# Layer 1's memory keys inside layer 0, the first retention values by token tile, sparse pairs ahead of the memory group

## The chip, the core and the metric

The kernel runs on one core of a Trainium2 chip. The metric is the device time of one execution in microseconds. Three runs of the kernel before gave 436.51 to 436.9 us, with a median of 436.82.

## What is computed

Two layers of a decoder over 256 positions (SEQ) with a model width of 1024, everything in float32. Layer 0 has three groups of heads beside each other: native sparse attention with 8 heads in two key groups (compressed blocks, selected blocks and a window; at 256 positions the selected blocks and the window both see all past tokens), block attention with 8 heads, and memory attention with 4 heads into 256 memory tokens. Layer 1 has retention with 4 heads (256 wide queries and keys, 512 wide values, a group norm over each head) and memory attention again. Each group has a gate path, each layer one output projection and a residual, and a final norm follows. Cut to what matters here:

```python
def memory_attention(q, mem_n, w_mem_kv):
    k, v = jnp.split(mem_n @ w_mem_kv, 2, axis=-1)
    ...
    s = jnp.einsum('bthd,bmhd->bhtm', q, k).astype(jnp.float32) * (HEAD_DIM ** -0.5)
    p = jax.nn.softmax(s, axis=-1).astype(v.dtype)
    return jnp.einsum('bhtm,bmhd->bthd', p, v).reshape(Bsz, T, MEM_W)
...
def odd_layer(x, mem_n, rcos, rsin, norm_g, w_in, w_mem_kv, w_out):
    h = rms_norm(x, norm_g)
    rq, rk, rv, rz, eq, ez = _split(h @ w_in, ODD_SPLITS)
    ...
    v = rv.reshape(Bsz, T, RET_HEADS, RET_V_DIM)
    r_out = head_group_norm(retention(q, k, v)).reshape(Bsz, T, RET_V_W).astype(x.dtype)
    m_out = memory_attention(eq.reshape(Bsz, T, MEM_HEADS, HEAD_DIM), mem_n, w_mem_kv)
```

The memory's keys and values of layer 1 depend on the memory and its weights alone, not on layer 0. The retention's values depend on x after layer 0 (called x1 below).

## The kernel before, in words

**Precision.** A float32 product is made of three matmuls in the format fp32r: the operand is split into a high part (ScalarE casts it, `whi`, line 122) and a low part (VectorE subtracts, `wlo`, line 123), and `mm3` (lines 135 to 137) adds high x high, high x low and low x high. `project_wide` (lines 181 and 182) does the same with two matmuls, of 512 and of 256 columns, for layer 1's turned projections.

**Weights.** They stream from memory through 6 buffers `raw` of 128 x 1024 numbers, loaded on SP's queue, and through 4 buffers each of `whi` and `wlo`. One buffer full is a unit; a projection of 512 columns has four units. A buffer comes free when the last matmul that reads it is done.

**Accumulators.** The eight PSUM banks are given out by tag: three for projections (`pj`), two for scores (`s`), one for transposes of probabilities (`t`), one for outputs of pairs (`o`) and one more (`tr`).

**Layer 0.** The projections run first, for the most part, each over both token tiles of 128 rows. Then come the pairs: a sparse pair has two heads and two branches, and a branch is a chain of scores (line 100), masked maximum and exponential (lines 415 and 417), division, three transposes per head (line 216), ScalarE's copy `pt` (line 430, or 476 for the memory group), and the product with the values (line 100). A pair ends with the gate (lines 441 to 443), which writes its part of the rows `yn`, `ym` or `yb` of the output projection. Five pieces of that projection, two units each, are taken as their rows are ready: `yn` of pairs 0 and 1, `ym`, `yn` of pairs 2 and 3, `yb` of block pairs 0 and 1 and of 2 and 3.

**Between the layers.** For each token tile and half of the columns, VectorE adds the residual (line 757) and multiplies by the norm's gain (line 759), TensorE transposes (line 216), ScalarE casts the high part (line 762) and VectorE subtracts the low part (line 763) of x1. Then `memory_keys1` projects the memory's keys and values for layer 1 (one projection of 512 columns of which the first 256 give the keys and the rest the values), and layer 1's memory queries and gate (`e1`) follow, the retention's queries and keys of heads 0 and 1, and for each head values (`rv`), gate (`rz`) and the retention itself.

**What sets the order.** The program is written in the order above, but a planner reorders it at build time: for every engine it takes, at each moment of its own model of the time, the first instruction in program order whose operands and buffers are ready. Each engine then runs its list strictly in order. `side_by_side` keeps a group of small matmuls together, and `after` lets the first of them wait for other instructions. In `pair_scores` these are the last reads of the scores before (`read`), except for sparse pair 2 and the memory group of layer 0 (`whole` is false). In `sparse_pair`, pair 2 alone gives its first branch's values to TensorE before the second branch is done.

## Time and profile before

| | us |
|---|---|
| median of three runs | 436.82 |
| profiled execution | 436.53 |
| its span, first to last instruction | 434.7 |
| TensorE busy (97% of the span) | 422.0 |
| TensorE's weight loads (81%, beside the matmuls) | 352.2 |
| VectorE busy (73%) | 315.3 |
| ScalarE busy (58%) | 250.5 |
| weights and inputs read | 72.74 MB |

The span is what the trace holds; the profiled execution is 1.8 us longer than that. In the trace's rows the engines are PE (TensorE), PEld (its weight loads), DVE (VectorE), ACT (ScalarE), POOL and SP, a row names the line of the kernel, the operation, what is written and read, and the shape. A matmul's time in such a row includes its way through the array, so that matmuls overlap: the pace is read from one start to the next. Two records stand for one float32 matmul of the pairs.

### The profile page before, as it was taken

How to read it: one execution, taken by the hardware profiler on the slowest of the kernel's cores; microseconds unless marked ns; L12 is line 12 of the kernel's file. 1: busy time of each engine (PE TensorE's matmuls, PEld its weight loads, DVE VectorE, ACT ScalarE, POOL GpSimd, SP SyncE). 2: the span in 40 equal slices, each digit the busy share in tenths (PEclk: the TensorE clock that was granted, in tenths of full speed). 3: DMA queues.
4: the chain of work that ended last, by engine and by line, in shares of the span. 5: the costliest groups of instructions: out<-in, count | busy, mean ns of one | idle time of the engine just before them, and what ended most of it. 6: DMA issues, size and time to landing. Idle time of an engine off the chain costs nothing.

```text
span 434.7 us, 6745 instructions
## 1 busy us (share of the span) xinstructions
PE 422.0 (97%) x2444; PEld 352.2 (81%) x2444; DVE 315.3 (73%) x735; ACT 250.5 (58%) x464; POOL 3.5 (1%) x9
## 2 busy tenths in 40 slices
PE   7999999999999998999999999999999999999994
PEld 6978999889777666669988878888888888888883
DVE  4889787798776786549688875596898557675634
ACT  5585546667858696647457534645445544644703
POOL 0000000000000000000000000000000000000001
PEclk9999999999999999999999999999999999999998
DMA  7975966763434623333663644555466455655202
GB/s 241 397 267 159 342 205 193 264 216 103 149 113 148 236 83 100 96 98 102 189 211 98 193 147 145 194 163 192 148 186 196 155 187 183 206 174 177 75 2 97
DMA packets 30337, 74.22 MB, mean 171 GB/s; under 512 B 2912, under 2 KB 14432, under 8 KB 30304
## 3 DMA queue, kind: packets, MB, share of 16 engines
q1 hardware_dynamic: 29872, 73.40, 51.7%
q8 instruction: 19, 0.31, 0.3%
q10 hardware_dynamic: 432, 0.40, 0.3%
q14 instruction: 14, 0.11, 0.1%
HBM read 72.74 MB, written 1.05 MB: 170 GB/s over the span
## 4 chain that ended last, share of the span: by engine, by line
PE 91%; DMA 4%; ACT 2%; DVE 1%; issue 1%; SPq 0%; DVEq 0%; ACTq 0%
PE pj L135 19%; PE pj L136 19%; PE pj L137 18%; PE pj L181 9%; PE pj L182 4%; PE t L216 4%; PE s L100 4%; PE o L100 3%; DMA raw<-in_w 2%; DMA v<-in_xtok 2%; PE tr L136 1%; PE tr L137 1%; PE tr L135 1%; PE s L136 1%; PE s L137 1%; PE s L135 1%
## 5 line engine op out<-in xcount | busy, mean ns | idle before, releaser
L123 DVE TENSOR_TENSOR wlo<-raw,whi 128x1024 fp32r<-128x1024 f32 (+3 forms) x127 | 147.3, 1166 | 58.9 <-ACT whi L122 57.4
L122 ACT CAST whi<-raw 128x1024 fp32r<-128x1024 f32 (+3 forms) x127 | 126.8, 1003 | 89.7 <-PE pj L137 39.8
L136 PE MATMUL pj<-wlo,big 128*128 128x512 f32 (+2 forms) x264 | 99.4, 377 | 0.0
L137 PE MATMUL pj<-whi,big 128*128 128x512 f32 (+2 forms) x264 | 98.3, 374 | 0.0
L135 PE MATMUL pj<-whi,big 128*128 128x512 f32 (+2 forms) x264 | 98.0, 375 | 0.0
L137 PEld LDWEIGHTS pj<-whi,big 128*128 128x128 f32 x264 | 49.7, 188 | 8.9 <-issue 0.7
L135 PEld LDWEIGHTS pj<-whi,big 128*128 128x128 f32 x264 | 49.6, 188 | 8.7 <-issue 0.4
L181 PE MATMUL pj<-big,whi 128*128 128x512 f32 x160 | 56.5, 396 | 0.0
L136 PEld LDWEIGHTS pj<-wlo,big 128*128 128x128 f32 x264 | 49.7, 188 | 8.4 <-issue 0.3
L182 PE MATMUL pj<-big,wlo 128*128 128x256 f32 x160 | 44.6, 283 | 0.0
L181 PEld LDWEIGHTS pj<-big,whi 128*128 128x128 f32 x160 | 29.8, 188 | 6.7 <-DVE tmp L365 0.3
L135 PE MATMUL pj<-big,whi 128*128 128x256 f32 x120 | 34.4, 290 | 0.1
L136 PE MATMUL pj<-big,whi 128*128 128x256 f32 x120 | 33.9, 285 | 0.0
L137 PE MATMUL pj<-big,wlo 128*128 128x256 f32 x120 | 33.2, 285 | 0.0
L182 PEld LDWEIGHTS pj<-big,wlo 128*128 128x128 f32 x160 | 30.2, 189 | 0.7 <-issue 0.3
L135 PEld LDWEIGHTS pj<-big,whi 128*128 128x128 f32 x120 | 23.0, 192 | 1.3 <-issue 0.7
L417 ACT ACTIVATE p<-p,mx 128x128 f32<-128x128 f32 (+1 forms) x48 | 21.4, 447 | 3.9 <-DVE mx L415 3.8
L136 PEld LDWEIGHTS pj<-big,whi 128*128 128x128 f32 x120 | 23.0, 192 | 0.1
L137 PEld LDWEIGHTS pj<-big,wlo 128*128 128x128 f32 x120 | 22.5, 191 | 0.0
L216 PE MATMUL t<-cst,p 128*128 128x128 f32 x104 | 17.9, 282 | 1.2 <-ACT pt L430 1.2
L216 PEld LDWEIGHTS t<-cst,p 128*128 128x128 f32 x104 | 11.8, 140 | 7.1 <-ACT pt L430 2.3
L430 ACT COPY pt<-t 128x384 f32<-128x384 f32 x24 | 11.4, 476 | 10.6 <-PE t L216 10.4
(302 smaller groups left out, 640.1 us busy)
## 6 DMA issues: line engine op xcount, KB each, us to landing
raw<-in_w SPq DMA_DIRECT2D x91, 512.0 KB, 4.2
raw<-in_wout SPq DMA_DIRECT2D x28, 512.0 KB, 3.8
v<-in_xtok SPq DMA_DIRECT2D x4, 512.0 KB, 8.2
raw<-in_w SPq DMA_DIRECT2D x4, 280.0 KB, 3.5
v<-in_w SPq DMA_DIRECT2D x2, 512.0 KB, 7.6
raw<-in_memT SPq DMA_DIRECT2D x2, 512.0 KB, 4.5
raw<-in_memtok SPq DMA_DIRECT2D x2, 512.0 KB, 4.8
v<-in_grow SPq DMA_DIRECT2D x2, 512.0 KB, 5.8
```

What stands on the lines that cost most here:

```text
L100: ins = PE.matmul(out, lhs, rhs, start=start, stop=stop, skip_group_check=bool(shared))
L122: S.copy(hi, raw)
L123: V.tensor_tensor(lo, raw, hi.bitcast(F32), ALU.subtract)
L135: PE.matmul(ps, lh, rh, start=start, stop=False, skip_group_check=shared)
L136: PE.matmul(ps, lh, rl, start=False, stop=False, skip_group_check=shared)
L137: PE.matmul(ps, ll, rh, start=False, stop=stop, skip_group_check=shared)
L181: PE.matmul(ps[ct], wh[:, c], both[:, :, kt], start=kt == 0, stop=False, skip_group_check=True)
L182: PE.matmul(ps[ct][:, T:], wl[:, c], both[:, 0, kt], start=False, stop=kt == KT - 1, skip_group_check=True)
L216: PE.transpose(b[:, i * P : (i + 1) * P], a, ident)
L417: S.activation(p[:, hh, a], p[:, hh, a], AF.Exp, bias=mx[:, hh, tok : tok + 1], scale=-1.0, accum_out=sm[:, hh, tok : tok + 1])
L430: got = S.copy(pt[:, hh, :384], transposes([p[:, hh, i * P : (i + 1) * P] for i in range(3)]))
```

## The change

1. The projection of layer 1's memory keys and values is cut in two halves of 256 columns (`project_half`, which loads half the columns of each weight row, in pieces of 1 KB). The keys (`memory_keys1`) move to the end of layer 0's program, behind the block pairs and ahead of the output projection. The values (`memory_values1`) stay where both were.
2. The retention's values of head 0 are projected right behind them, ahead of `e1`, and token tile by token tile: `project_rows` splits all four units, then runs tile 0 over all of the depth, then tile 1. The other heads' values keep their place and form.
3. Sparse pair 3 moves ahead of the memory group and the last two block projections. In every sparse pair both branches' values go to TensorE in one group, and every pair's scores wait for the last read of the scores before.
4. The output projection of layer 0 takes the piece of sparse pairs 2 and 3 ahead of the memory group's.

```diff
--- before.py
+++ after.py
@@ -165,6 +165,19 @@
             turned_unit(ps, lhs, wh, wl, (kt, kt + 1), range(4))
         return ps
 
+    def project_rows(src, idx, lhs, cols=512):
+
+        hi, lo = lhs
+        ps = [bank("pj") for _ in range(2)]
+        ws = list(units(src, idx, cols))
+        for tok in range(2):
+            ts = slice(tok * P, (tok + 1) * P)
+            for k0, wh, wl in ws:
+                for j in range(2):
+                    cs = slice(j * cols, (j + 1) * cols)
+                    mm3(ps[tok], hi[:, k0 + j, ts], lo[:, k0 + j, ts], wh[:, cs], wl[:, cs], k0 + j == 0, k0 + j == KT - 1)
+        return ps
+
     def project_wide(src, idx, both):
 
 
@@ -200,6 +213,29 @@
                     c = slice(j * 512 + 256, j * 512 + 512)
                     mm3(ps[1][:, tok * T : (tok + 1) * T], hi[:, kt, ts], lo[:, kt, ts], wh[:, c], wl[:, c],
                         kt == 0 and tok == 0, kt == KT - 1, True)
+        return ps
+
+    def halves(src, idx, half):
+
+        for u in range(2):
+            raw = load(tl("raw", [P, 1024], NRAW),
+                       src[idx + u].rearrange("p (k c) -> p k c", k=4)[:, :, half * 256 : half * 256 + 256])
+            wh, wl = split(raw, 1024)
+            for j in range(4):
+                yield 4 * u + j, wh[:, j * 256 : (j + 1) * 256], wl[:, j * 256 : (j + 1) * 256]
+
+    def project_half(src, idx, lhs, half):
+
+        hi, lo = lhs
+        ps = bank("pj")
+        for kt, wh, wl in halves(src, idx, half):
+            for i in range(2):
+                c = slice(i * P, (i + 1) * P)
+                out = ps[:, i * T : (i + 1) * T]
+                if half == 0:
+                    mm3(out, wh[:, c], wl[:, c], hi[:, kt], lo[:, kt], kt == 0 and i == 0, kt == KT - 1, True)
+                else:
+                    mm3(out, hi[:, kt, c], lo[:, kt, c], wh, wl, kt == 0 and i == 0, kt == KT - 1, True)
         return ps
 
     def spread(col, dst):
@@ -397,11 +433,11 @@
 
     read = []
 
-    def pair_scores(q, k, spans, whole=True):
+    def pair_scores(q, k, spans):
 
         s = [bank("s") for _ in range(2)]
         side_by_side([(s[hh][:, a], q[pair_half(hh), tok * P : tok * P + P], k[pair_half(hh), : a.stop - a.start], True, True)
-                      for tok, a in enumerate(spans) for hh in range(2)], *(read if whole else ()))
+                      for tok, a in enumerate(spans) for hh in range(2)], *read)
         read.clear()
         return [[s[hh][:, a] for a in spans] for hh in range(2)], s
 
@@ -456,7 +492,7 @@
             pt = tl("pt", [P, 2, 512], 2)
             mx = tl("mx", [P, 2, 2], 3)
             sm = tl("sm", [P, 2, 2], 3)
-            _, ss = pair_scores(eqT[:, pr], kT[:, pr], WHOLE, together)
+            _, ss = pair_scores(eqT[:, pr], kT[:, pr], WHOLE)
             for hh in range(2):
                 s = ss[hh]
                 V.tensor_reduce(mx[:, hh], s.rearrange("p (a k) -> p a k", a=2), AX.X, ALU.max, negate=True)
@@ -596,14 +632,11 @@
         PE.matmul(o[:, :T], vcR[:, pr % 2].rearrange("p g f -> p (g f)"), pcT[:, pr // 2], start=True, stop=False)
         todo, done = [], []
         for br in (1, 2):
-            pt, got = causal_weights(pair_scores(nq[:, pr], kS[:, br - 1], SPAN, pr not in (2,))[0],
+            pt, got = causal_weights(pair_scores(nq[:, pr], kS[:, br - 1], SPAN)[0],
                                      gates[:, :, br * 8 + 2 * pr : br * 8 + 2 * pr + 2])
             todo += causal_values(pt, lambda g, kt, br=br: vsw[:, kt, (br - 1) * P + g * 64 : (br - 1) * P + g * 64 + 64],
                                   o, False, br == 2)
             done.append(got)
-            if br == 1 and pr not in (0, 1, 3):
-                side_by_side(todo, *done)
-                todo, done = [], []
         side_by_side(todo, *done)
         gated(o, szn[:, pr], yn, pr)
 
@@ -681,10 +714,16 @@
             gated(o[:, i * T : (i + 1) * T], szb[:, pr], yb, pr)
 
     def memory_keys1():
-        nonlocal mh, ml, rstdm, rbm, k1m, v1m
+        nonlocal k1m
         k1m = tl("s2", [P, 2, T], NS)
+        scaled(project_half(w512, W["m1"], (mh, ml), 0), rbm, 1.0, k1m)
+
+    def memory_values1():
+        nonlocal v1m
         v1m = tl("s2", [P, 2, T], NS)
-        mem_keys(project_mem(w512, W["m1"], (mh, ml)), rstdm, rbm, k1m, v1m)
+        ps = project_half(w512, W["m1"], (mh, ml), 1)
+        for tok in range(2):
+            S.activation(v1m[:, tok], ps[:, tok * T : (tok + 1) * T], AF.Copy, scale=rstdm[:, tok : tok + 1])
 
 
     sparse_keys()
@@ -695,18 +734,18 @@
     block_gates()
     block_keys()
     memory_rows()
-    for pr in range(3):
+    for pr in range(4):
         sparse_pair(pr)
     memory_scale()
     memory_keys()
     memory_group()
     block_queries()
     block_values()
-    sparse_pair(3)
     block_pairs(0)
     block_pairs(1)
     block_pairs(2)
     block_pairs(3)
+    memory_keys1()
 
 
     def part(acc, tok, c0, n, y, k, wh, wl, start, stop):
@@ -742,7 +781,7 @@
 
     x0 = [load(tl("v4", [P, D], NV), xtok[:, tok]) for tok in range(2)]
     g1 = load(tl("v4", [P, D], NV), grow[0:1].to_broadcast([P, D]))
-    acc = out_project([(1, yn, 0), (0, ym, 0), (2, yn, 2), (3, yb, 0), (4, yb, 2)])
+    acc = out_project([(1, yn, 0), (2, yn, 2), (0, ym, 0), (3, yb, 0), (4, yb, 2)])
 
 
     x1 = tl("big", [P, 2, KT, T], 2, F32R)
@@ -774,8 +813,19 @@
     V.scalar_tensor_tensor(str_[:, 0], sn[:, 64:], -1.0, rb1, op0=ALU.mult, op1=ALU.mult)
     V.tensor_tensor(str_[:, 1], sn[:, 64:], rb1, ALU.mult)
 
-
-    memory_keys1()
+    def ret_v(h, how):
+        ps = how(w512, W[f"rv{h}"], (x1h, x1l))
+        vh = tl("v4", [P, 2, 512], NV, F32R)
+        vl = tl("v4", [P, 2, 512], NV, F32R)
+        for tok in range(2):
+            r = rstd1[:, tok : tok + 1]
+            S.activation(vh[:, tok], ps[tok], AF.Copy, scale=r)
+            V.scalar_tensor_tensor(vl[:, tok], ps[tok], r, vh[:, tok].bitcast(F32), op0=ALU.mult, op1=ALU.subtract)
+        return vh, vl
+
+
+    memory_values1()
+    vs = [ret_v(0, project_rows)]
     wide_e = project_wide(w512, W["e1"], x1)
     eqS1 = tl("s2", [P, 2, T], NS)
     szm1 = tl("s2", [P, 2, T], NS)
@@ -834,13 +884,7 @@
         if h % 2 == 0:
             qs = ret_qk(f"rq{h // 2}")
             kks = ret_qk(f"rk{h // 2}")
-        ps = project(w512, W[f"rv{h}"], (x1h, x1l))
-        vh = tl("v4", [P, 2, 512], NV, F32R)
-        vl = tl("v4", [P, 2, 512], NV, F32R)
-        for tok in range(2):
-            r = rstd1[:, tok : tok + 1]
-            S.activation(vh[:, tok], ps[tok], AF.Copy, scale=r)
-            V.scalar_tensor_tensor(vl[:, tok], ps[tok], r, vh[:, tok].bitcast(F32), op0=ALU.mult, op1=ALU.subtract)
+        vh, vl = vs.pop(0) if vs else ret_v(h, project)
         ps = project(w512, W[f"rz{h}"], (x1h, x1l))
         sz = tl("v4", [P, 2, 512], NV)
         for tok in range(2):
```

## The prediction

> **What bounds the kernel now.** I read the page first: the share of each engine and the chain that ended last.
>
> ```profile
> span 434.7 us, 6745 instructions
> PE 422.0 (97%) x2444; PEld 352.2 (81%) x2444; DVE 315.3 (73%) x735; ACT 250.5 (58%) x464; POOL 3.5 (1%) x9
> ...
> PE 91%; DMA 4%; ACT 2%; DVE 1%; issue 1%; SPq 0%; DVEq 0%; ACTq 0%
> ```
>
> TensorE is busy for 422.0 of 434.7 us and 91% of the chain is TensorE's. The change adds and removes almost no matmul, so it can only act on the 12.7 us in which TensorE is idle. The second view, busy time by stretch, says where these lie (columns: stretch, length, then busy us of PE, PEld, DVE, ACT, POOL, granted clock, DMA share, GB/s).
>
> ```profile
> 50.00:138.60 88.60, 88.56 (x647) 76.89 (x646) 70.01 (x194) 56.89 (x128) 0.84 (x2) 1.00 0.56 184
> 138.60:149.00 10.40, 10.40 (x66) 7.41 (x64) 6.79 (x12) 7.57 (x18) 0.00 (x0) 1.00 0.77 263
> 149.00:158.00 9.00, 7.76 (x65) 4.94 (x64) 7.61 (x35) 8.16 (x27) 0.00 (x0) 1.00 0.44 149
> 158.00:174.00 16.00, 14.81 (x92) 10.65 (x91) 10.63 (x42) 11.50 (x34) 0.00 (x0) 1.00 0.22 68
> 174.00:197.40 23.40, 22.08 (x126) 15.62 (x124) 12.56 (x33) 12.22 (x30) 0.00 (x0) 1.00 0.30 90
> 197.40:210.70 13.30, 13.29 (x112) 13.29 (x113) 12.47 (x25) 9.21 (x16) 0.00 (x0) 1.00 0.52 159
> 226.00:424.00 198.00, 198.00 (x965) 164.55 (x966) 139.24 (x277) 102.78 (x145) 0.00 (x0) 1.00 0.49 158
> 424.00:434.70 10.70, 4.52 (x32) 4.00 (x30) 4.85 (x12) 3.44 (x11) 2.05 (x1) 0.81 0.26 98
> ```
>
> 6.2 us belong to the tail after the last output projection, which the change doesn't touch. Layer 1 from 226 us on has none, nor has the stretch from 50 to 149 us. The only idle time within reach is 1.24 + 1.19 + 1.32 = 3.75 us between 149 and 197.4 us, where the attention pairs of layer 0 end and the first output projection runs between them. The third view, TensorE's waits in that stretch, names the cause (columns: who waits for whom, us in total, times, longest), and the timeline of TensorE three of its places (start, us, what; in brackets the idle time before it).
>
> ```profile
> PE t L216 <- ACT pt L430: 1.2, 2, 0.6
> PE o L100 <- ACT pt L476: 0.7, 1, 0.7
> ```
>
> ```profile
> 150.31 0.55 PE L216 MATMUL t<-cst,p 128*128 128x128 f32 x3
> 151.42 0.87 PE L100 MATMUL o<-pt,s 128*64 128x256 f32 x8 [0.57 <-ACT pt L430]
> ...
> 170.85 0.49 PE L216 MATMUL t<-cst,p 128*128 128x128 f32 x3
> 172.52 1.52 PE L100 MATMUL o<-pt,s 128*64 128x256 f32 x16 [1.19 <-ACT pt L430]
> ...
> 175.31 0.55 PE L216 MATMUL t<-cst,p 128*128 128x128 f32 x3
> 175.61 0.48 PE L135 MATMUL pj<-whi,y 128*128 128x512 f32 x1
> ```
>
> The reader is to see five waits of the same kind, two in brackets (151.42 and 172.52), one and two in the rows above: probabilities are transposed (t), ScalarE copies them (pt), and TensorE has no projection left to run until the copy is done. Three transposes that a projection follows take 0.30 us from start to start (175.31 to 175.61). At 150.31 they take 1.11 until the next start and at 170.85 1.67, so by starts these two cost 0.81 and 1.37 us, 0.2 more than the idle time in brackets. The wait for pt of line 476 (memory group, 0.7) comes to 0.9 in this way, and the two of transposes (1.2 in all) to 0.8 each. The first, the memory group's and that at 172.5 lie before 174 us and cost 3.1 us together, some 2.8 if each leaves an ordinary switch of 0.1; the other two, between block pairs, come after 174.
>
> **The change part by part.** *Matmuls.* Layer 1's memory keys and values are 96 matmuls of 256 columns before and 48 + 48 after; the retention values are 48 of 512 columns in either order. The price of one comes from starts in the boundary between the layers:
>
> ```profile
> 194.59 0.39 PE L136 MATMUL pj<-wlo,y 128*128 128x512 f32 x1
> ...
> 196.89 0.39 PE L137 MATMUL tr<-whi,y 128*128 128x512 f32 x1
> 197.41 0.39 PE L135 MATMUL pj<-big,whi 128*128 128x256 f32 x1
> ...
> 202.29 0.60 PE L216 MATMUL t<-cst,tmp 128*128 128x128 f32 x4
> 202.65 0.37 PE L136 MATMUL pj<-wlo,big 128*128 128x256 f32 x1
> 202.85 0.60 PE L216 MATMUL s<-cst,tmp 128*128 128x128 f32 x4
> ...
> 207.85 0.28 PE L135 MATMUL pj<-big,whi 128*128 128x256 f32 x1
> ...
> 209.29 0.28 PE L135 MATMUL pj<-whi,big 128*128 128x256 f32 x1
> ```
>
> Twelve matmuls of 256 columns take 1.44 us (207.85 to 209.29), 0.12 each, so each half of the memory projection is 48 x 0.12 = 5.8 us. Ten of 512 columns take 2.30 us (194.59 to 196.89), 0.23 each, so one token tile of the retention values is 24 x 0.23 = 5.5 us. The sum over the kernel is unchanged: 0.
>
> *The keys' half inside layer 0.* 5.8 us of matmuls that wait for nothing in the pairs become cover for the stretch that lacks it. It stands ahead of the output projection in program order, so it is drawn on first, once the last block projection is through (about 138.6 us), and the output pieces of pairs 0 and 1, which now are gone by 149 us, last 5.8 us longer. That carries the cover across the wait at 150.3 and the memory group's. That at 170.9 stands where the pieces of pairs 2 and 3 come late; with all sparse pairs ahead of the memory group both are ready before it, so I take this too as gone. The two after 174 us lie between block pairs, each of which frees one piece only; nothing there is changed, and I keep them. Bounds: 0 gone, or all five (4.7 us). I take the three: **-2.8 us**. If the cover is not there, the price is these 2.8 us back.
>
> Its own costs: it will be cut up by the pairs' transposes. One matmul between two groups took 0.20 instead of 0.12 (202.65 to 202.85), so four cuts are +0.3. Two loads move ahead on SP's queue, two ScalarE casts and two VectorE subtractions (1.05 and 1.22 us each, rows below) move with them; weights are loaded six buffers ahead and TensorE never waits for a load in this stretch. ScalarE is 91% busy from 149 to 158 us, so the two casts cost there if they fall there; they have 138 us before it in which to be early, and I take 0, with 2.1 us as the upper end.
>
> *Sparse pairs.* Pair 2's values go in one group of 16 instead of two of 8 (1.52 against 2 x 0.87 in the rows above): -0.2. Its scores and those of the memory group now wait for the last read of the score banks. The other sparse pairs wait for it already, and TensorE's waits hold none of that kind: 0. Pair 3 and the memory group change places among the same four block projections; that stretch has 0.04 us of idle time in 88.6.
>
> *The boundary.* Here the change takes away what it gave: from 197.4 us only 5.8 us of matmuls, not 11.5, run while VectorE makes x1. The retention values of tile 0 then need only tile 0 of x1. VectorE's timeline tells when that is ready (tile 0's two halves come from the banks t and s, tile 1's last from o), and ScalarE's group of the weight casts what one of them takes (count, busy us, mean ns):
>
> ```profile
> 203.54 1.22 DVE L123 TENSOR_TENSOR wlo<-raw,whi 128x1024 fp32r<-128x1024 f32 x1
> ...
> 205.34 0.68 DVE L763 TENSOR_TENSOR big<-s,big 128x512 fp32r<-128x512 f32 x1
> ...
> 207.81 0.69 DVE L763 TENSOR_TENSOR big<-o,big 128x512 fp32r<-128x512 f32 x1
> ```
>
> ```profile
> L122 ACT CAST whi<-raw 128x1024 fp32r<-128x1024 f32 x11 | 11.6, 1052 | 8.2 <-PE tr L137 5.4 <-PE pj L137 2.6
> ```
>
> Tile 0 is whole at 205.34 + 0.68 = 206.0, tile 1 at 208.5. TensorE comes to the end of the values' half and the four groups of transposes at 197.41 + 5.8 + 4 x 0.44 (0.36 and a switch) = 204.9. So it waits 1.1 us, and everything of layer 1 is behind it in TensorE's queue. After that tile 0 gives 5.5 us, to 211.5, and tile 1 (208.5) is hidden; the token order is what keeps the wait from being 208.5 - 204.9 = 3.6. Bounds: 0, since one weight split (203.54) stands ahead of the two subtractions and the planner could put it behind them, and 3.6 if two splits more are put ahead (1.1 + 2 x 1.22). I take **+1.1**, the order as it is.
>
> *Buffers.* The token order holds four split weights at once, all of the four buffers, so layer 1's query weights can be split only when the second pass lets go of its first unit, 1.4 us into 5.5. Cast and subtraction take 2.3 us: hidden, with 1.8 us to spare; with that gone the price is what exceeds it. The values' evacuation needs the row scales, which follow x1's squares on VectorE; the second pass covers them. The 11 us leave the place between the keys and the gate of head 0, where TensorE has no idle time on either side: 0.
>
> **Sum.** -2.8 + 0.3 - 0.2 + 1.1 = -1.6 us. The profiled execution took 436.53 us, of which 434.7 are the span; that gives 434.9. The median of the three runs is 0.3 above that execution, so I expect **435.2** for the median.
>
> **The rivals.** *Slower: the cover is spent where nothing was uncovered.* The keys' half is available from 138.6 us, and from there to 149 TensorE is 10.40 of 10.40 busy already. If the planner puts all of it there and the output pieces don't move back by as much, the five waits stay and the boundary pays 1.1 to 3.6 us for lost cover. At +1.2 (1.1 + 0.3 - 0.2) the time is 438.0. For it: work from 138.6 to 149 was used up at once before, and ScalarE, which the waits name, has no more time than before. Against it: the same pieces run later if something runs ahead of them. It decides once the boundary's wait exceeds the waits removed by 0.9 us.
>
> On the clock the Trainium skill ("TensorE: Matmul & The Clock Gate", Part 1) says that an idle window of about 3.4 us puts the array back to half speed until it has been busy as long again. In the trace the clock is 1.00 through all waits of up to 1.2 us, and 0.81 only in the tail, which agrees. By that rule the upper end of 3.6 us at the boundary would cost about 1.7 us more, an estimate from the page's window: 439.7 plus what the waits left. No run so far shows it.
>
> *No change: gain and loss cancel,* or the change doesn't do what it says: the planner orders by its own times, and could leave the keys' half at the end of layer 0, next to the values' half, as it is now. Then the order on TensorE is nearly that of before: 436.8. For it: the half has the last place ahead of the output projection. Against: it waits for nothing, and list order lets it in at the first hole.
>
> *Better: all five waits go and x1 comes in time.* 436.82 - 4.7 + 0.1 = 432.2. For it: the block pairs would each have a spare output piece if the cover lasts. Against: the two late waits stand where transposes of one pair follow each other, with the copy between them, and pieces come singly.
>
> **How the numbers follow.** A change of 0.2% (0.9 us) is about what a measurement of this kernel can tell from none. Forecast (435.2, its own range 434.2 to 436.2) 0.47; slower 0.19; no change 0.24; better 0.10. Faster by more than 0.2% means below 435.95: most of the forecast's case and all of the better one, 0.42 + 0.10 = 0.52. Within 0.2%: 0.24 and the forecast's rest, 0.29. Slower 0.19. The range for 8 in 10 leaves out the upper half of the slower case and two thirds of the better one: 433.2 to 438.2.
>
> **What would show it.** Right: in the changed kernel TensorE's waits for pt between the end of the block projections and the boundary come down from 3.7 us to about 1.3, matmuls into pj from the memory rows stand in that stretch, and at the boundary there is one wait of about 1 us for VectorE's x1 ahead of the retention values. Wrong on the cover: the waits for pt are as long as now. Wrong on the boundary: no wait there, or one of over 2 us, with weight splits between the subtractions of x1. The prediction as a whole fails if TensorE's idle time outside the tail isn't what moved, for instance if matmuls between groups become slower or the stretch before 138.6 us opens up.

## The result, and the profile after

The changed kernel takes **433.5 us** (median of eight runs, 433.02 to 435.32) against 436.25 for the kernel before in eight runs beside it (435.55 to 436.9): a ratio of 0.9947, with a 95% interval of 0.9934 to 0.9961. It is 0.5% faster. The forecast was 435.2 with a range of 433.2 to 438.2: right in sign, 1.7 us too high. The median of before over these eight runs is 0.6 us under that of the three runs that the forecast started from, so 1.1 of the 1.7 us is gain that was not foreseen: 2.75 us instead of 1.6. One execution each of three kernels further down took 697.89, 1463.2 and 2362.25 us; these three are left out of all medians and ratios.

The page of the profiled execution (434.82 us) begins with the span, the busy time of each engine, and the engines' shares in the chain that ended last:

```profile
span 433.0 us, 6745 instructions
PE 420.4 (97%) x2444; PEld 351.3 (81%) x2444; DVE 314.8 (73%) x735; ACT 250.9 (58%) x464; POOL 3.5 (1%) x9
...
PE 94%; ACT 2%; DMA 2%; DVE 1%; SPq 0%; issue 0%; DVEq 0%; ACTq 0%
```

TensorE still bounds the kernel, with as many matmuls as before and the same share of the span. The two profiled spans differ by 1.7 us. To see where, I cut them at three matmuls that both kernels have: the first scores of layer 0, the last matmul of its output projection, and the last matmul of all. These are TensorE's rows, of the kernel before and then of the changed one (the row of before that is missing, 196.89, stands in the prediction):

```profile
81.60 0.49 PE L100 MATMUL s<-s,v 64*128 64x128 f32 x4
...
428.24 0.28 PE L137 MATMUL s<-v,y 128*128 128x256 f32 x1
```

```profile
82.37 0.49 PE L100 MATMUL s<-s,v 64*128 64x128 f32 x4
...
201.76 0.39 PE L137 MATMUL tr<-whi,y 128*128 128x512 f32 x1
...
426.66 0.28 PE L137 MATMUL s<-v,y 128*128 128x256 f32 x1
```

| stretch (us) | before | after | after - before |
|---|---|---|---|
| start to first scores | 81.60 | 82.37 | +0.8 |
| first scores to the end of layer 0 ("the stage") | 115.3 | 119.4 | +4.1, with 5.76 us of keys' matmuls moved in: **-1.7** net |
| end of layer 0 to the last matmul ("layer 1") | 231.35 | 224.90 | -6.45, with the same 5.76 moved out: **-0.7** net |
| after it | 6.5 | 6.3 | -0.1 |

The first stretch holds nothing that the change touches. What differs there is TensorE's pace. The eight matmuls that start at 5.17 us in both take 1.87 us by starts in before and 1.05 in the changed kernel's execution, though the profile gives a clock of 1.00 for both there. Behind them the granted clock of the latter (its share of full speed) is 0.50 from 11.5 to 14.5 us, while that of before is 1.00 there. Other executions below differ by as much in either direction. So the change gave 1.7 + 0.7 = 2.4 us in this pair of traces and 2.75 in the medians.

Busy time by stretch, with the columns that the prediction explained, shows what became of the 3.75 us of idle time in the stage:

```profile
139.10:158.00 18.90, 18.90 (x138) 15.23 (x137) 11.89 (x34) 12.25 (x32) 0.00 (x0) 1.00 0.62 208
158.00:174.00 16.00, 14.87 (x103) 10.50 (x103) 12.20 (x43) 13.46 (x40) 0.00 (x0) 1.00 0.31 100
174.00:202.20 28.20, 26.95 (x156) 18.86 (x152) 16.27 (x45) 15.95 (x40) 0.00 (x0) 1.00 0.31 94
202.20:209.30 7.10, 7.01 (x59) 7.01 (x60) 7.03 (x13) 6.01 (x13) 0.00 (x0) 1.00 0.44 135
209.30:226.00 16.70, 16.70 (x86) 14.11 (x85) 12.94 (x27) 9.48 (x13) 0.00 (x0) 1.00 0.49 152
```

From 139.1 to 158 us there is no hole any more. Then 1.13 and 1.25 us are left, 2.38 in all. TensorE's waits give them the name they had, ScalarE's copy `pt` (its line is 466 now):

```profile
PE t L252 <- ACT pt L466: 1.8, 3, 0.6
...
PE o L100 <- ACT pt L466: 0.6, 1, 0.6
```

From 202.2 us, the boundary between the layers, TensorE is busy but for 0.09 us: there is no wait for x1. TensorE's timeline has both places:

```profile
139.15 0.28 PE L135 MATMUL pj<-big,whi 128*128 128x256 f32 x1
...
148.62 0.40 PE L135 MATMUL pj<-whi,y 128*128 128x512 f32 x1
...
162.54 0.39 PE L137 MATMUL tr<-whi,y 128*128 128x512 f32 x1
...
164.68 0.55 PE L252 MATMUL t<-cst,p 128*128 128x128 f32 x3 [0.56 <-ACT pt L466]
165.79 1.52 PE L100 MATMUL o<-pt,s 128*64 128x256 f32 x16 [0.57 <-ACT pt L466]
...
202.29 0.39 PE L135 MATMUL pj<-whi,big 128*128 128x256 f32 x1
...
209.00 0.60 PE L252 MATMUL s<-cst,tmp 128*128 128x128 f32 x4
209.36 0.48 PE L135 MATMUL pj<-whi,big 128*128 128x512 f32 x1
209.68 0.39 PE L136 MATMUL pj<-wlo,big 128*128 128x512 f32 x1
209.91 0.60 PE L252 MATMUL o<-cst,tmp 128*128 128x128 f32 x4
210.26 0.48 PE L137 MATMUL pj<-whi,big 128*128 128x512 f32 x1
```

The keys' half (`pj` from the memory's rows in `big`, 256 columns) starts right behind the last block projection and is through at 148.6 us. The first output pieces (`y`) last from there to 162.54 instead of to 149. Behind them the next two waits come, where there were none before. At the boundary the values' half starts at 202.29 and the retention values follow at 209.36.

### The profile page after: what moved, and what is told of

Its sections match the earlier page's. It is cut to its first block, busy times and chain, and to the rows that moved or that the text cites. A ratio compares the mean times of both kernels' runs of the same rounds, so it can differ in the third digit from the quotient of the medians.

```text
span 433.0 us, 6745 instructions
## 1 busy us (share of the span) xinstructions
PE 420.4 (97%) x2444; PEld 351.3 (81%) x2444; DVE 314.8 (73%) x735; ACT 250.9 (58%) x464; POOL 3.5 (1%) x9
## 3 DMA queue, kind: packets, MB, share of 16 engines
HBM read 72.74 MB, written 1.05 MB: 170 GB/s over the span
## 4 chain that ended last, share of the span: by engine, by line
PE 94%; ACT 2%; DMA 2%; DVE 1%; SPq 0%; issue 0%; DVEq 0%; ACTq 0%
PE pj L135 19%; PE pj L137 19%; PE pj L136 19%; PE pj L194 9%; PE pj L195 4%; PE t L252 4%; PE s L100 4%; PE o L100 3%; DMA raw<-in_w 2%; PE s L135 1%; PE s L136 1%; PE s L137 1%; PE tr L135 1%; PE tr L137 1%; PE tr L136 1%; PE s L852 1%
## 5 line engine op out<-in xcount | busy, mean ns | idle before, releaser
L195 PE MATMUL pj<-big,wlo 128*128 128x256 f32 x160 | 44.7, 282 | 0.0
L135 PE MATMUL pj<-big,whi 128*128 128x256 f32 x120 | 35.0, 295 | 1.5 <-ACT whi L122 1.5
L194 PEld LDWEIGHTS pj<-big,whi 128*128 128x128 f32 x160 | 29.9, 188 | 7.2 <-DVE wlo L123 0.3
L136 PE MATMUL pj<-big,whi 128*128 128x256 f32 x120 | 34.7, 291 | 0.0
L137 PE MATMUL pj<-big,wlo 128*128 128x256 f32 x120 | 34.0, 293 | 0.0
L135 PEld LDWEIGHTS pj<-big,whi 128*128 128x128 f32 x120 | 23.4, 196 | 2.8 <-ACT whi L122 1.7
L136 PEld LDWEIGHTS pj<-big,whi 128*128 128x128 f32 x120 | 23.5, 196 | 0.2
L135 PE MATMUL pj<-whi,y 128*128 128x512 f32 x42 | 16.9, 407 | 0.0
```

The lines of the kernel that those rows point to most:

```text
L135: PE.matmul(ps, lh, rh, start=start, stop=False, skip_group_check=shared)
L136: PE.matmul(ps, lh, rl, start=False, stop=False, skip_group_check=shared)
L137: PE.matmul(ps, ll, rh, start=False, stop=stop, skip_group_check=shared)
L194: PE.matmul(ps[ct], wh[:, c], both[:, :, kt], start=kt == 0, stop=False, skip_group_check=True)
L195: PE.matmul(ps[ct][:, T:], wl[:, c], both[:, 0, kt], start=False, stop=kt == KT - 1, skip_group_check=True)
```

## The experiments

All times are medians; a ratio is to the kernel before on the same chip, with its 95% interval. The changed kernel itself was run again beside them twice: 433.97 against 436.1 (0.9942, 0.9925 to 0.9959) and 433.55 against 436.8 (0.9924, 0.9912 to 0.9937). "Stage" and "layer 1" are cut as in the table above.

| kernel | us | ratio (interval) | stage | layer 1 |
|---|---|---|---|---|
| changed | 433.97, 433.55 | see above | 119.4 | 224.9 |
| 1 retention values back in their place | 438.16 | 1.0038 (1.0022 to 1.0053) | 119.5 | 227.9 |
| 2 keys' half at the boundary | 435.02 | 0.9973 (0.9959 to 0.9986) | 114.75 | 230.45 |
| 3 pairs as before | 434.29 | 0.9952 (0.9938 to 0.9967) | 120.4 | 224.9 |
| 4 keys' half left out | 430.14 | 0.9867 (0.9848 to 0.9887) | 115.6 | 224.9 |
| 5 retention values early, ordinary order | 433.79 | 0.9946 (0.9930 to 0.9963) | 119.4 | 224.9 |
| 6 retention values early, nothing else | 435.04 | 0.9973 (0.9960 to 0.9986) | 115.2 | 230.5 |
| 7 values' half in another bank | 435.65 | 0.9993 (0.9982 to 1.0005) | 121.65 | |
| 8 pair 3's values in two groups | 433.68 | 0.9930 (0.9913 to 0.9947) | 119.3 | |
| 9 column halves of x1 swapped | 433.36 | 0.9932 (0.9907 to 0.9957) | 119.4 | 224.95 |
| 10 before, with one group kept whole | 435.75 | 0.9983 (0.9971 to 0.9995) | 115.3 | 230.7 |

**The changed kernel again.** The two repetitions say how far a difference between two kernels can be read.

> The changed kernel once more, on the chip of the three that follow, as their base. Expected: 2.0 to 2.8 us below the kernel before (its trace has TensorE's waits for pt at 2.4 us instead of 3.7, and no wait for x1 at the boundary).

> The changed kernel as the base of the three that follow, on their chip: 0.993 to 0.996 of the kernel before.

The ratios 0.9942 and 0.9924 and the first 0.9947 overlap; a tenth of a per cent more or less between two variants is nothing that these runs can tell.

**1. Retention values back in their place.** The keys' half stays in layer 0, and the pairs keep their new order.

```diff
-    vs = [ret_v(0, project_rows)]
+    vs = []
```

> The changed kernel with head 0's retention values back in their old place and order, so that after the memory values' half only layer 1's query weights are left to run. Theory (token order pays for the boundary): the queries' first four depth tiles need the first half of x1's second token tile, which VectorE finished 3.0 us after the values' half ended in the changed kernel (212.9 against 209.9 us), so one wait of 2.5 to 3.6 us at the boundary and a time as much above the changed kernel, that is no faster than the kernel before. Rival (x1 would come in time anyway once the planner knows of the need): a wait under 1 us, within 0.8 us of the changed kernel.

This kernel is **slower than before**, by 0.2 to 0.5%, and 4.2 us slower than the changed one. (From the first scores to the last matmul its trace is 0.8 us longer than that of before.) TensorE's timeline, VectorE's, and the busy time of one stretch:

```profile
208.42 0.60 PE L252 MATMUL o<-cst,tmp 128*128 128x128 f32 x4
211.94 0.50 PE L194 MATMUL pj<-big,whi 128*128 128x512 f32 x1 [2.92 <-DVE big L802]
```

```profile
209.98 1.23 DVE L123 TENSOR_TENSOR wlo<-raw,whi 128x1024 fp32r<-128x1024 f32 x1 [0.46 <-ACT whi L122]
211.20 0.69 DVE L802 TENSOR_TENSOR big<-s,big 128x512 fp32r<-128x512 f32 x1
```

```profile
209.00:212.00 3.00, 0.08 (x2) 0.07 (x1) 2.50 (x7) 1.93 (x4) 0.00 (x0) 1.00 0.55 170
```

Here is the wait that the prediction priced at 3.6 us for a boundary where tile 1 of x1 is needed at once: 2.92 us idle for the first half of tile 1's low part (211.20 + 0.69 = 211.89). Four transposes take 0.36 us, so by starts it costs 211.94 - 208.42 - 0.36 = 3.2. Layer 1 is 3.0 us longer in the traces (227.9 against 224.9). The medians say 4.2. For the last 1 us the record has a hint: the profiled execution (436.9) and one other (436.1) had a mean granted clock of 0.996 and 0.997, the remaining ten (437.75 to 439.65) one of 0.989 to 0.994; the six of the changed kernel beside them had 0.995 to 0.998. A clock lower by 0.003 over 435 us comes to some 1.3 us, an estimate from these figures and an upper one, since the means include the tail, where TensorE has nothing left to do. Where in those ten executions the clock was lower, at the boundary or elsewhere, is not shown, since only the one at 436.9 left a trace. A weight split of 1.23 us stands ahead of the subtraction, the order that the prediction took. So what pays for the boundary is the early place of the retention values.

**2. Keys' half at the boundary.** Early values and the new order of pairs stay; layer 0 has no extra work.

```diff
     block_pairs(3)
-    memory_keys1()
...
+    memory_keys1()
     memory_values1()
```

> The changed kernel with the memory keys' half at the boundary, right ahead of the values' half; pairs and retention values as changed. Theory (the keys' half is cover in layer 0): waits for pt between the block projections and the boundary rise to 3.7 us or more, and the time is 1.3 to 2.5 us above the changed kernel. Rival (the order of the pairs took the waits away): waits for pt as in the changed kernel, 2.4 us, and the time within 0.5 us of it.

It takes 1.05 us more than the changed kernel beside it. The stage is 4.65 us shorter for the 5.76 that left it, so in layer 0 the keys' half cost 4.65 and hid 1.1. TensorE's waits tell which holes it fills:

```profile
PE t L252 <- ACT pt L466: 2.2, 4, 0.6
...
PE o L100 <- ACT pt L466: 1.1, 2, 0.6
```

3.3 us instead of 2.4: one wait of each kind more. No more than these two come back: both the waits and the time stay below what was expected (3.7 us or more, and 1.3 to 2.5 us).

**3. Pairs as before.** Sparse pair 3 behind the memory group, pair 2's values in two groups, the old order of output pieces; keys' half and early values stay (three of its lines):

```diff
-    for pr in range(4):
+    for pr in range(3):
...
     block_values()
+    sparse_pair(3)
...
-    acc = out_project([(1, yn, 0), (2, yn, 2), (0, ym, 0), (3, yb, 0), (4, yb, 2)])
+    acc = out_project([(1, yn, 0), (0, ym, 0), (2, yn, 2), (3, yb, 0), (4, yb, 2)])
```

> The changed kernel with the sparse pairs, the pieces of the output projection and the grouping of pair 2 as before; keys' half and retention values as changed. Theory (the keys' half is the cover): within 0.8 us of the changed kernel. Rival (the order of the pairs took the waits away): 1.3 us or more above the changed kernel, with waits for pt of 3.7 us.

By time it can't be told from the changed kernel (0.9952 against 0.9942). The trace is clearer: the stage is 1.0 us longer. TensorE's waits in the stage, from its timeline:

```profile
158.99 1.08 PE L100 MATMUL o<-pt,s 128*64 128x256 f32 x8 [0.68 <-ACT pt L512]
...
176.52 1.52 PE L100 MATMUL o<-pt,s 128*64 128x256 f32 x16 [1.19 <-ACT pt L466]
...
184.44 0.55 PE L252 MATMUL t<-cst,p 128*128 128x128 f32 x3 [0.57 <-ACT pt L466]
194.07 0.55 PE L252 MATMUL t<-cst,p 128*128 128x128 f32 x3 [0.62 <-ACT pt L466]
```

Of the five waits of before, the keys' half alone removes one: the first, at 151.4. The memory group's (0.68) and pair 3's long one (1.19) are still there, 5.1 us later when counted from the first scores. The new order of pairs is what trades 0.68 + 1.19 for the 0.56 + 0.57 at 164.7 and 165.8.

**4. Keys' half left out**, to have its price from the other side. Layer 1 uses layer 0's memory keys instead, so this kernel doesn't compute the two layers.

```diff
-        nonlocal k1m
+        nonlocal k1m, memk
         k1m = tl("s2", [P, 2, T], NS)
-        scaled(project_half(w512, W["m1"], (mh, ml), 0), rbm, 1.0, k1m)
+        V.tensor_copy(k1m, memk)
```

> The changed kernel with the projection of layer 1's memory keys left out (layer 1 uses layer 0's memory keys instead), so 48 matmuls, 5.8 us of TensorE's time, are gone from layer 0. This gives the net price of those 5.8 us. Theory (they are cover and fill about 1.4 us of waits, as leaving them at the boundary showed): the time falls by only 4.0 to 4.8 us against the changed kernel, to 0.983 to 0.985 of the kernel before, and waits for pt are back at 3.3 us or more. Rival (they lie beside nothing): it falls by 5.8 us, to 0.981.

It takes 0.9867 of before, the changed kernel 0.9942 and 0.9924: the keys' half costs 2.5 to 3.3 us by these, less than the 4.0 to 4.8 expected. The stage is 3.8 us shorter, and it has six waits of the kind instead of four: the four that the changed kernel has too, and ahead of them two that it lacks, in TensorE's timeline:

```profile
149.63 0.55 PE L252 MATMUL t<-cst,p 128*128 128x128 f32 x3 [0.52 <-ACT pt L466]
150.75 1.52 PE L100 MATMUL o<-pt,s 128*64 128x256 f32 x16 [0.57 <-ACT pt L466]
```

The 5.76 us of matmuls cover 1.1 us of holes. This trace also holds a wait of 0.74 us for a weight split at 81.9 that the others lack; without it the stage would be shorter by about that, and the price of the keys' half in the stage some 4.6 us, as in run 2. The medians put it lower, with an interval of about 1 us on either side.

**5. Retention values early, in the ordinary order** (`project`, which takes both token tiles unit by unit).

```diff
-    vs = [ret_v(0, project_rows)]
+    vs = [ret_v(0, project)]
```

> The changed kernel with head 0's retention values in their new place but in the ordinary order, both token tiles after each unit of the weights. Its second dozen of matmuls needs the first half of x1's second token tile, which in the changed kernel is ready 3.5 us after the retention values start (212.9 against 209.4), and the first dozen takes 1.4 us less than half of that. Theory (the token order is what hides x1): one wait of 1.5 to 2.5 us at the boundary for x1, and the time as much above the changed kernel, 0.998 to 1.000 of the kernel before. Rival (the new place alone does it): no wait over 0.5 us, within 0.6 us of the changed kernel.

The same time (0.9946 against 0.9942), and the same stages. In its trace TensorE runs tile 0 over nearly all units before tile 1, though the program has both tiles unit by unit: the planner takes what is ready. (The rows don't name the tile; ScalarE empties tile 0's accumulator at 214.90 us and tile 1's at 220.36, 5.5 us apart, as in the changed kernel.) The token order written out isn't what helps.

**6. Retention values early, and nothing else**: the kernel before, with the memory projection in its two halves, both at the boundary.

```diff
     memory_keys1()
+    memory_values1()
+    vs = [ret_v(0, project_rows)]
     wide_e = project_wide(w512, W["e1"], x1)
...
-        ps = project(w512, W[f"rv{h}"], (x1h, x1l))
...
+        vh, vl = vs.pop(0) if vs else ret_v(h, project)
```

> The kernel before with one part of the change alone: head 0's retention values right after the memory's keys and values of layer 1 (both halves at the boundary), by token tile. There TensorE had no wait for x1 and none in layer 1. Theory (only waits move the time): within 0.5 us of the kernel before. Rival (the new order of layer 1 is itself shorter, by fewer breaks between groups; from the boundary to the end the changed kernel takes 0.8 us less than the kernel before with the keys' half taken off): 0.6 to 1.2 us below the kernel before, without any difference in the waits.

1.2 us faster than before (0.9973), though no wait at the boundary was there to be removed. The stage is as long as before (115.2), and layer 1 is 0.9 us shorter. This is a gain that the prediction had at zero; run 10 looks for it.

**7. Values' half in another accumulator bank.** The keys' half runs ahead of the output projection as a whole, and the values' half behind it as a whole; here the values' half writes the bank `o`, and the last transposes of x1 move to `pj` (one of the lines):

```diff
-        ps = project_half(w512, W["m1"], (mh, ml), 1)
+        ps = project_half(w512, W["m1"], (mh, ml), 1, "o")
```

> A version that may be better: the memory values' half gathers in the bank of the pairs' outputs, which is free at the boundary, instead of in a projection bank that VectorE must first empty; the last transposes of x1 take a projection bank in exchange. In the changed kernel TensorE stands for 0.3 us more than a switch between the output projection and that half (0.53 us from start to start, where 0.23 is the matmul). Theory: 0.2 to 0.4 us below the changed kernel. Rival: the planner's order elsewhere changes and the time differs by more, either way; or 0.

By the ratios it is 2 to 3 us slower than the changed kernel, so it gives back nearly all of the gain. The planner did pull the free half forward, but to the wrong place:

```profile
198.24 0.39 PE L137 MATMUL tr<-whi,y 128*128 128x512 f32 x1
198.47 0.28 PE L135 MATMUL o<-whi,big 128*128 128x256 f32 x1
...
200.86 0.40 PE L135 MATMUL pj<-whi,y 128*128 128x512 f32 x1
```

```profile
PE pj L252 <- DVE tmp L798: 1.2, 1, 1.2
```

Twenty of its matmuls (198.47 to 200.86, 2.4 us) went ahead of the last output piece. All of x1 then came later, and TensorE waited 1.2 us for its last product with that much less cover in hand. VectorE had also put two weight splits in a row (2.35 us from 206.65) ahead of that product.

**8. Pair 3's values in two groups**, for the waits at 164.7 and 165.8: its first branch's values are given to TensorE before the second branch is done.

```diff
             done.append(got)
+            if br == 1 and pr == 3:
+                side_by_side(todo, *done)
+                todo, done = [], []
```

> A version that may be better: the changed kernel, but sparse pair 3 gives its first branch's values to TensorE before the second branch is done. In the changed kernel two waits for pt of 0.8 and 0.7 us (by starts) stand around 164 us, where pair 3's second branch is transposed, and its first branch's eight matmuls (0.80 us) are ready before. Theory (waits are filled by whatever is ready): one of the two waits is filled, at the price of one more break of 0.15 us, and the time is 0.4 to 0.8 us below the changed kernel. Rival (the chain of copies on ScalarE sets the pace there): the waits move or stay, and the time is within 0.3 us or above.

No difference (0.9930 against 0.9924). One wait goes (1.2 us in two instead of 1.8 in three of that row), the other stays at 0.57, and a new one of 0.21 for the memory group's copy stands behind it; TensorE's busy time from 156 to 172 us is 15.22 of 16. ScalarE is busy for 13.96 of those 16 us, which fits that its copies set the pace here; that they do is argued, not shown.

**9. Column halves of x1 swapped**, to test why the boundary has no wait. In the changed kernel the third matmul of the retention values is the first that reads x1's low part, and it reads a depth slice of the first column half. With the second half made first, it needs both.

```diff
-        for c in range(2):
+        for c in (1, 0):
```

> The changed kernel with the two column halves of x1 made in the other order, for both token tiles. The retention values begin with depth tiles 0 to 3, which are the first half; that is now made second. Theory (the boundary shows no wait in the changed kernel because only the first half of token tile 0 is needed at the start, and the second 2.7 us later): TensorE waits 0.5 to 1.2 us for x1 ahead of the retention values, and the time is as much above the changed kernel. Rival (tile 0 is needed whole, as the prediction had it, and there was room for it): no new wait and the same time within 0.3 us.

No difference in time, and no wait either. TensorE's rows and VectorE's (the bank `t` holds the first half, now made second):

```profile
208.38 0.60 PE L252 MATMUL s<-cst,tmp 128*128 128x128 f32 x4
208.80 0.50 PE L137 MATMUL pj<-whi,big 128*128 128x512 f32 x1
```

```profile
208.06 0.68 DVE L802 TENSOR_TENSOR big<-t,big 128x512 fp32r<-128x512 f32 x1
```

The whole of tile 0 is ready at 208.06 + 0.68 = 208.74, and needed at 208.80. That the first half alone suffices is so in the changed kernel, but it isn't why the wait is absent.

**10. Before, with one group kept whole.** Runs 6 and 2 left layer 1 shorter by 0.9 us. The largest difference between the traces at one place is in layer 1's memory group. TensorE's rows of before, and then of the changed kernel:

```profile
231.59 0.27 PE L216 MATMUL t<-cst,p 128*128 128x128 f32 x1
231.79 0.70 PE L100 MATMUL s<-s,s 64*128 64x256 f32 x2
232.42 0.55 PE L216 MATMUL t<-cst,p 128*128 128x128 f32 x3
232.90 1.13 PE L100 MATMUL s<-s,s 64*128 64x256 f32 x6
233.96 0.38 PE L182 MATMUL pj<-big,wlo 128*128 128x256 f32 x1
```

```profile
240.80 0.60 PE L252 MATMUL t<-cst,p 128*128 128x128 f32 x4
241.15 0.48 PE L194 MATMUL pj<-big,whi 128*128 128x512 f32 x1
...
242.37 1.14 PE L100 MATMUL s<-s,s 64*128 64x256 f32 x8
243.44 0.49 PE L194 MATMUL pj<-big,whi 128*128 128x512 f32 x1
```

Four transposes and eight scores stand mixed as 1, 2, 3, 6 in before and take 233.96 - 231.59 = 2.37 us. Apart, as 4 and 8, with projection matmuls around them, they take 0.35 + 1.07 = 1.42. The experiment is the kernel before with nothing but this undone: the second pair's scores wait for the copy of the first transposes.

```diff
                 got = S.copy(pt[:, hh], transposes(...))
+                if together and pr == 0 and hh == 0:
+                    read.append(got)
```

> The kernel before with one more dependency: in layer 1's memory group the second pair's scores wait for the copy of the first pair's first transposes. In the kernel before these four transposes and eight scores are mixed on TensorE (1 + 2 + 3 + 6, 2.37 us from 231.59 to 233.96); in the changed kernel they stand apart (0.35 and 1.07 us). Theory (most of the 0.9 us by which layer 1 became shorter with the early retention values is this mixing, not waits): 0.5 to 1.0 us below the kernel before, 0.9977 to 0.9988 of it. Rival (the 0.9 us come from many small breaks all along layer 1): within 0.3 us of the kernel before.

Its timeline has them apart, and layer 1 is 0.7 us shorter than in before (427.01 - 196.34 = 230.67 against 231.35); the time is 0.9983 of before, 0.7 us.

```profile
234.79 0.60 PE L216 MATMUL t<-cst,p 128*128 128x128 f32 x4
235.32 1.13 PE L100 MATMUL s<-s,s 64*128 64x256 f32 x8
```

The two groups, one behind the other, take 1.59 us here (234.79 to the next matmul at 236.38), 0.78 less than when mixed. So 0.7 of the 0.7 to 0.9 us in layer 1 come from a group that the new order happened to leave whole. The 0.2 by which the other runs go beyond it isn't settled.

No run that computes the two layers was clearly faster than the changed kernel; run 5 equals it with less code.

## Why the prediction was right or wrong

**The keys' half as cover: right in kind, over-sized.** The step was "I take the three: -2.8 us", less 0.3 for cuts and 0.2 more from the grouping, 2.7 in all. Measured: 1.7. The sentence that failed is "That carries the cover across the wait at 150.3 and the memory group's". Alone, the keys' half carried it across the first wait only (run 3) and gained 5.76 - 5.1 = 0.7 us; with the new order of pairs it gained 1.1 (runs 2 and 4). The rest is the pairs' order, 0.5 without the keys' half (115.2 to 114.75, run 6 to run 2) and 1.0 with it (run 3), not the 0.2 forecast for it; only the traces show that part, the times of runs 2 and 6 are equal. The wait at 170.9 did go, as forecast, but pair 3, now earlier, brought two of its own, at 164.7 and 165.8. There the output pieces had run out (162.54): each piece needs two pairs, and the one that pair 3 completes can't cover pair 3 itself.

The prediction held 5.8 us of cover against waits of 3.1. What counts is not how much there is but whether any is left at the hour of the wait. All 48 matmuls ran between 139.15 and 148.62, ahead of the first hole, and the output pieces that they pushed back were used up by 162.54, although only some 1 us of cover was needed up to there. The two late waits between block pairs stayed, as forecast (0.57 and 0.62, at 185.33 and 194.96 in the changed kernel). So the idle time came down from 3.75 us to 2.38, not to 1.3.

Why the values' half isn't taken for these holes I can only argue: the output projection's accumulators hold all three `pj` banks and `tr` until it ends. Run 7, where a bank was free, fits, but there the half went ahead of the output projection's end instead of into the two block waits.

**The boundary: wrong by 1.1 us, the pieces nearly right.** The step was "So it waits 1.1 us". "No wait there" was its own condition for being wrong, and there is none. In the changed kernel TensorE reads x1's low part first at 210.26, and VectorE's rows say when that was there:

```profile
208.91 0.68 DVE L802 TENSOR_TENSOR big<-t,big 128x512 fp32r<-128x512 f32 x1
209.58 0.68 DVE L802 TENSOR_TENSOR big<-s,big 128x512 fp32r<-128x512 f32 x1
```

Two terms were off by about half a microsecond each, and both to the good. Measured from the start of the values' half, tile 0 was whole at 209.58 + 0.68 - 202.29 = 8.0 us, not 206.0 - 197.4 = 8.6. And the prediction had the retention values stop at their first matmul, after 204.9 - 197.4 = 7.5 us; but the first two of the three matmuls of each product (lines 135 and 136) read x1's high part only, which ScalarE's cast gives before VectorE subtracts. The third, behind them and the last group of transposes, came at 210.26 - 202.29 = 8.0. Run 9 shows the match with both halves needed: ready at 208.74, used at 208.80. That is a slack of 0.06 us; in the changed kernel, where the first half suffices, it is 210.26 - 209.59 = 0.7. That "the token order is what keeps the wait from being" 3.6 is wrong as put: run 5 does without it. The early place is what keeps it (run 1: 3.2 by starts).

On the clock: through the idle time of 2.92 us in run 1 the granted clock stays at 1.00 (its row above). The Trainium skill ("TensorE: Matmul & The Clock Gate", Part 1), cited in the prediction, sets the idle window at about 3.4 us; a wait of 2.92 below it leaves the clock alone, which agrees. No trace here has a longer wait at the boundary; the ten executions of run 1 with a lower mean clock have none. But a single wait's length isn't all that counts. In the profiled execution of the changed kernel the clock went to 0.50 at 11.5 us, and the longest wait before that was 1.48 us; in its second repetition a wait of 1.81 at the same matmul left the clock at 1.00. What decided there isn't shown.

**The early retention values: "0", wrong by 0.7 to 0.9 us in the good direction.** The step was that the change "can only act on the 12.7 us in which TensorE is idle": the prediction looked at idle time in layer 1, found none, and took layer 1 for fixed. But TensorE's busy time held 0.8 to 0.95 us in one mixed group (run 10). Its last condition, that something other than idle time moved, came true for a quarter to a third of the gain.

**Terms that held.** Loads, casts and subtractions of the moved half cost nothing that shows: TensorE is 18.90 of 18.90 busy from 139.1 to 158 us. The second pass covers the query weights: 16.70 of 16.70 from 209.3 to 226.

**The rivals.** "Cover spent where nothing was uncovered" is not what happened to the whole, but what happened to most of the keys' half: 5.76 us moved and 0.7 to 1.1 hidden. With the retention values in their old place its direction holds, and its price at the boundary, but not its layer 0: run 1 has the changed kernel's four waits for pt there (2.3 us), not five. That its time, 438.16, lies so near the 438.0 of that rival is chance. "No change" fell: keys' half and early values stand elsewhere on TensorE. "Better" had x1 in time, which came true, and all five waits gone, which did not.

**The sum.** Stage -1.7 instead of -2.7, boundary 0 instead of +1.1, layer 1 -0.7 instead of 0: -2.4 instead of -1.6. The errors of the first two terms, +1.0 and -1.1, cancel, which is luck; the 0.7 of layer 1 is most of the gain that was missed. With the cover as measured and the boundary as forecast the sum would have been -0.6, less than the 0.9 that the prediction called measurable.

## What to carry to other kernels

Filler work is worth what is still left of it at the hour of each wait: list the waits with their times, run the list of free work against them, and expect a scheduler that takes the first ready instruction to spend it as soon as it can, holes or not. Before work that covered a boundary is taken away, put there what needs the late operand last or only in part, and price the boundary without it: here it decides between 0.5% faster and 0.4% slower. And a bound engine at 97% is not at its floor: small matmuls that the planner mixed are busy time which another order gives back.

## What the runs showed of the hardware

- **Mixed groups of small matmuls.** Four transposes and eight scores of 64 rows took 2.37 us when mixed as 1, 2, 3 and 6, 1.59 as two whole groups one behind the other (run 10), and 1.42 as two whole groups apart (the changed kernel). Undoing this alone gave 0.7 us (run 10). The profile counts all of it as busy time.
- **The start differs between executions** of one kernel before any of the changed code runs: the first scores of the changed kernel start at 82.37, 80.76 and 81.45 us in its three traces, 1.6 us apart. The first of these is the one whose clock was 0.50 from 11.5 to 14.5 us; in the other two it was 1.00 there. A difference of single profiled spans below 1.6 us says little, and the cut at common matmuls is what made the stages comparable.
